# A two-layer decoder trunk on one core: when the first weight sums of a phase are fetched and split, and where two splits stand in a unit

## The chip, the cores and the metric

The kernel runs on one core of one Trainium2 chip. The metric is device time in microseconds, the median of several executions. The core has five engines that run side by side, each through its own instructions in a fixed order: TensorE (PE, matmuls), VectorE (DVE), ScalarE (ACT), GpSimd (POOL) and SyncE (SP). SP and POOL start DMA transfers here; an instruction that waits holds up everything behind it on its engine.

## The reference

The reference is a two-layer decoder trunk in float32 for one sequence of 256 tokens and a model width of 2048. Each layer has a token mixer and a gated MLP. The change lies in the MLP alone, which is

```python
h    = rmsnorm(x)
gate, val = h @ W_up                  # 2048 -> 2 x 5632
gate = silu(causal_conv3(gate))
y    = (gate * val) @ W_down          # 5632 -> 2048
x    = x + rmsnorm(y)
```

## The kernel before

**Precision.** PE multiplies a rounded float32. Each operand is therefore split in two: ACT copies it rounded into `hi` (L600), and DVE subtracts `hi` from it to give `lo` (L601). A product is three matmuls: hi·hi, lo·hi and hi·lo (`mm3`, L127). Weights arrive by DMA as float32 in a tile `raw` (three buffers for all uses) and are split into `whi` and `wlo` (four buffers each); the split's last subtraction lets the raw buffer go.

**The MLP of a layer.** The 5632 hidden columns are 11 groups of 512. Group 0 is done plainly (`narrow(0)`). Groups 1, 3, 5, 7 and 9 (`WIDE`) go through five wide phases per layer; each phase does two things side by side.

1. `wide` computes the two up projections of its group with seven products in place of eight (a Strassen scheme): L127 with the accumulators `ps_g` and `ps_s`. It runs over eight *units* (two 128-row blocks of the model width each). A unit needs four forms of weights. Two are plain and come from a 768 KB transfer `raw` (L637, from `uw`); `plain` splits them into `fa` (1024 columns) and `fb` (512 columns). Two are sums. The first sum `d` (`first_sums`, L606 and L607) is made by the transfer itself: SP loads 512 KB into a tile `sh`, and when that has landed POOL starts a second transfer of 512 KB that adds onto it. The second sum `e` is made by DVE from `d` and `raw` (L643, L644). Both are split into the four tiles called `x` (one buffer; L600 and L601 with `x<-sh`).
2. `beside` supplies one tile b of the plain up projection of the next group per unit (`ws_beside`, L155 to L175): a 1 MB transfer into `raw`, two splits of 1024 columns, two half sweeps of 16 matmuls (L162) into one PSUM bank, and then a copy on ACT (L174) and an addition on DVE (L175) that empty the bank. The first half sweep of the next tile cannot start before L175.

PE's order in unit u is fixed: first half sweep of b(u), products 1, 2 and 3 (9 matmuls, on `fa` and `fb`), second half sweep, products 7, 5, 6 and 4 (12 matmuls, on `x`). Instructions passed through `pin` keep the order in which the code issues them.

**Between phases** `downs` multiplies two finished groups by their down weights: eight 1 MB pieces (`dn`) of 24 matmuls each. The four results per layer half are stored to `yout` by POOL (from the second time on by an adding transfer, L764). In the middle of it `early(i)` requests the first sums of units 0 and 1 of the next phase. In phase 1 the request comes from `narrow(0)`, ahead of its second half.

Inside `wide`, unit u's code issues the loads and sums of unit u+1, and requests the first sums of unit u+2. Work left over from other parts (the convolution, SiLU and the gating) is called at `catch_up`.

**Order of the rest.** What is not pinned is placed by a scheduler, which works from the order of the code and its own costs; each engine's list is fixed once built. The list of an engine names tiles with a running number.

Of the kernel before, what the change touches and what calls it, by code (L numbers as in the profile page):

```python
# [10 lines left out]
F32 = mybir.dt.float32  # L11
# [25 lines left out]
WIDE = (1, 3, 5, 7, 9)  # L37
# [8 lines left out]
class Body:  # L46
    def __init__(self, ctx, tc, a):
        self.tc, self.nc, self.a = tc, tc.nc, a
        self.sb = ctx.enter_context(tc.tile_pool(name="sb", bufs=1))
        self.todo = []  # L50
        self.pinned, self.behind = False, []
        self.psp = ctx.enter_context(tc.tile_pool(name="ps", bufs=1, space=bass.MemoryType.PSUM))
        self.outside = ctx.enter_context(tc.tile_pool(name="outside", bufs=1, space=bass.MemoryType.DRAM))

# [45 lines left out]
    def piece(self, src, cuts=1, store=None, between=None):  # L100


        nc = self.nc
        raw = self.sb.tile([P, 2048], F32, name="raw", tag="raw", bufs=3)
        n = 2048 // cuts
        for h in range(cuts):
            dma = nc.sync.dma_start(raw[:, h * n:(h + 1) * n], src[:, h * n:(h + 1) * n])
            if cuts > 1:
                self.tc.keep_in_program_order(dma)
            if h == 0 and between:  # L110
                between()
        res = []
        n = min(n, 1024)
        for h in range(2):
            if store:
                hi, lo = (v[:, h * 1024:(h + 1) * 1024] for v in store)
            else:
                hi = self.sb.tile([P, 1024], F32R, name="whi", tag="whi", bufs=4)
                lo = self.sb.tile([P, 1024], F32R, name="wlo", tag="wlo", bufs=4)
            for i in range(0, 1024, n):  # L120
                r, ns = raw[:, h * 1024 + i:h * 1024 + i + n], slice(i, i + n)
                self.split(hi[:, ns], lo[:, ns], r)
            res.append((hi, lo))
        return res

    def mm3(self, out, lhi, llo, rhi, rlo, start, stop):
# [98 lines left out]
    def sums(self, n):  # L225

        ss = self.sb.tile([P, n, 5], F32, name="sums", tag="sums", bufs=2)
        self.nc.gpsimd.memset(ss[:, :, 4:5], EPS)
        return ss
# [367 lines left out]
        return s, make  # L597

    def split(self, hi, lo, of):
        self.pin(self.nc.scalar.copy(hi, of))  # L600
        self.pin(self.nc.vector.tensor_sub(lo, of, hi.bitcast(F32)))  # L601

    def first_sums(self, src, u):

# [3 lines left out]
                                 src[u][:, 1536:].unsqueeze(1).to_broadcast([P, 2, 512]), accum_op=ALU.add)  # L608
        return d

    def wide(self, src, ahead, h, s, forms, r, beside):

        nc, n = self.nc, KT // 2  # L620
        ps = {i: self.bank("g" if i in (1, 2, 6, 7) else "s") for i in range(1, 8)}
        pin, add = self.pin, nc.vector.tensor_add
        half = lambda f, i: f[..., i * 512:(i + 1) * 512]

        def lhs(i, u):
            if i in (1, 2, 4):
                kt, t = 2 * u + (i != 1), int(i == 4)
                return [h[2][:, kt, a, t * P:(t + 1) * P] for a in range(2)]
            return [s[:, u, {5: 0, 6: 1, 7: 2, 3: 3}[i], a, :] for a in range(2)]

        def product(i, u, f, at):
            self.mm3(ps[i], *lhs(i, u), half(f[0], at), half(f[1], at), u == 0, u == n - 1)

        def load(u):

            raw = self.sb.tile([P, 2048], F32, name="raw", tag="raw", bufs=3)
            nc.sync.dma_start(raw[:, :1536], src[u][:, :1536])  # L637
            return raw

        def sums(d, raw):  # L640

            e = self.sh([P, 1024])
            pin(add(half(e, 1), half(d, 0), half(raw, 2)))  # L643
            pin(add(half(e, 0), half(e, 1), half(raw, 0)))  # L644
            return d, e

        def plain(raw):
            fa, fb = ([self.sb.tile([P, 1024], F32R, name=k, tag=k, bufs=4) for k in ("whi", "wlo")]
                      for _ in range(2))
            self.split(*fa, raw[:, 0:1024])  # L650
            self.split(*(half(f, 0) for f in fb), half(raw, 2))
            return fa, fb

        summed = [[forms[:, 2 * i + j, :] for j in range(2)] for i in range(2)]

        def split_sums(t):
            for of, parts in zip(t, summed):
                self.split(*parts, of)

        raw = load(0)  # L660
        t = sums(ahead.pop(0), raw)
        split_sums(t)
        b = beside[0]()
        next(b)
        next(b)
        f = plain(raw)
        self.pinned = True
        for u in range(n):
            more = u + 1 < n
            next(b)  # L670
            if u:
                split_sums(t)
            self.catch_up()
            fa, fb = f
            product(1, u, fa, 1)
            product(2, u, fa, 0)
            product(3, u, fb, 0)
            if more:
                raw = load(u + 1)
                if u + 2 < n:  # L680
                    ahead.append(self.first_sums(src, u + 2))
                t, f = sums(ahead.pop(0), raw), plain(raw)
            self.catch_up()
            if more:
                after = beside[u + 1]()
                next(after)
            next(b)
            next(b, None)
            if more:
                next(after)  # L690
            product(7, u, summed[0], 1)
            product(5, u, summed[0], 0)
            product(6, u, summed[1], 1)
            product(4, u, summed[1], 0)
            b = after
        a, g0, v0, v1 = (self.sc([P, 512]) for _ in range(4))
        more = lambda out, x, i: pin(add(out, ps[i], x))

        def scaled(out, i, t):
            pin(nc.vector.scalar_tensor_tensor(out, ps[i], r[:, t:t + 1], out, op0=ALU.mult, op1=ALU.add))  # L700

        pin(nc.scalar.copy(a, ps[1]))
        pin(nc.scalar.activation(g0, ps[1], AF.Copy, scale=r[:, 0:1]))
        scaled(g0, 2, 0)
        more(a, a, 6)
        more(v0, a, 5)
        more(v0, v0, 3)
        more(a, a, 7)
        more(v1, a, 5)
        pin(nc.scalar.activation(a, a, AF.Copy, scale=r[:, 1:2]))  # L710
        scaled(a, 4, 1)
        self.pinned = False
        self.catch_up(-1)
        return (g0, a), (v0, v1)

    def ffn(self, layer, h, each, filler=None, done=None, late=None):
        nc = self.nc
        up, uw, dn = (self.a["%s%d" % (k, layer)] for k in ("up", "uw", "dn"))
        r, R = {}, []
# [23 lines left out]
        yout = self.outside.tile([4, P, 1024], F32, name="yout", tag="yout", bufs=1)  # L743
        acts, ahead = {}, []

        def early(i):
            ahead[:] = [self.first_sums(uw[i], u) for u in range(2)]

        def downs(groups):

            lhs = [p for b in groups for p in acts[b]]
            for c0 in (0, 2):
                banks = {c: [self.bank(), self.bank()] for c in (c0, c0 + 1)}
                for pi, b in enumerate(groups):
                    for c in banks:
                        self.as_piece(banks[c], dn[c, b:], lhs, pi, at=0)
                        if pi == 1:
                            y = self.sh([P, 1024])
                            for t in range(2):
                                nc.scalar.copy(y[:, t * 512:(t + 1) * 512], banks[c][t])  # L760
                            if 0 in groups:
                                nc.gpsimd.dma_start(yout[c], y)
                            else:
                                nc.gpsimd.dma_start(yout[c], y, accum_op=ALU.add)  # L764
                if c0 == 0:
                    early(WIDE.index(groups[1] + 1))

        def weights(ft):
            return [self.cols[:, cv + i * NFT + ft:cv + i * NFT + ft + 1] for i in range(4)]
# [58 lines left out]

        def narrow(g):
            for p in (2 * g, 2 * g + 1):  # L830
                if p % 2:
                    early(0)
                w = place(p)
                ga = self.ws_pair(up[w, 0], h)
                if p == 0:

                    val = self.ws_pair(up[w, 1], h)
                gate(ga)
                c, steps = conv(p, ga)
                at_once(steps)  # L840
                if p:
                    val = self.ws_pair(up[w, 1], h)
                at_once(keep(p, c, val))
# [46 lines left out]
        self.behind_this(*(lambda i=i: rest(i) for i in range(5, KT // 2 + 1)))  # L890
        forms = self.sb.tile([P, 4, 1024], F32R, name="x", tag="x", bufs=1)
        for g in WIDE:
            made = self.wide(uw[WIDE.index(g)], ahead, h, s, forms, R[0], beside(g + 1))
            for i in range(2):
                self.later(2 + i, lambda made=made, g=g, i=i: turned(g, made, i))
            if g < WIDE[-1]:
                downs((max(g - 2, 0), g + 1))
# [300 lines left out]
```

## Time and profile before

| | before |
|---|---|
| timed runs, us | 2294.56, 2297.04, 2300.41 (median 2297.04) |
| profiled execution, us | 2287.66 |
| its span, first to last instruction, us | 2285.9 |
| mean granted clock of PE | 0.986 |
| PE busy, us | 2212.9 (97%), 10962 matmuls |
| DVE busy, us | 1659.3 (73%) |
| ACT busy, us | 1304.1 (57%) |
| DMA moved | 516.78 MB, mean 226 GB/s |

How to read it: PE is the busiest engine by far, but its busy time is modelled and stretches with the clock, so what it waits for matters more than the share. A row of a timeline gives start, duration, engine, source line, operation, output and inputs, how often, and in square brackets the idle time before it and what ended that. A row of waits gives the waiting group, what released it, the total, the number of waits and the longest. In a row of windows the column after the length is PE's busy time, and the last three are the granted clock (1.00 is full), the busy share of the 16 DMA engines, and GB/s. A DMA row gives the issuing queue, the number of transfers, the size of one, and the median time from issue to landing.

### The profile page before, as it was taken

What the parts mean: (1) busy time and instruction counts of PE and PEld (TensorE: products, weight loads), DVE (VectorE), ACT (ScalarE), POOL (GpSimd) and SP (SyncE); (2) the same over time, 40 slices, a digit from 0 to 9 for tenths busy, and PEclk for the clock granted to TensorE, in tenths of its full rate; (3) what the DMA queues carried; (4) which work ended last, traced back from release to release, by engine and by line L of the source; (5) the groups of instructions that cost most, each with busy time, mean ns of one, the idle gap of its engine ahead of it and who ended that gap; (6) DMA issues with size and microseconds to landing.
All of it is one profiled execution on the core that took longest, in us unless ns stands there. A gap on an engine that the chain in (4) does not pass through costs nothing.

```text
span 2285.9 us, 28964 instructions
## 1 busy us (share of the span) xinstructions
PE 2212.9 (97%) x10962; PEld 1853.1 (81%) x10962; DVE 1659.3 (73%) x2175; ACT 1304.1 (57%) x1844; POOL 149.4 (7%) x168
## 2 busy tenths in 40 slices
PE   9999999999998999999999999999999999999998
PEld 7888888788787877778888888887877778787786
DVE  6567767987767858678864667579858678586786
ACT  7556556666555555556664555466555556555563
POOL 0000000101001010010000000001010010100100
PEclk9999999999999999999999999999999999999999
DMA  8755456877969688697755444658788786886974
GB/s 320 265 171 188 165 182 216 248 236 260 263 219 264 211 260 249 202 282 259 249 175 193 155 166 159 215 192 258 225 263 236 216 264 218 249 251 201 269 248 182
DMA packets 102380, 516.78 MB, mean 226 GB/s; under 512 B 10464, under 2 KB 10848, under 8 KB 61920
## 3 DMA queue, kind: packets, MB, share of 16 engines
q1 hardware_dynamic: 72288, 439.43, 54.3%
q0 software_dynamic: 29952, 75.51, 16.3%
q8 instruction: 86, 1.41, 0.2%
q14 instruction: 54, 0.44, 0.1%
HBM read 491.82 MB, written 23.07 MB: 225 GB/s over the span
## 4 chain that ended last, share of the span: by engine, by line
PE 79%; DMA 12%; DVE 4%; issue 2%; ACT 2%; SPq 0%; POOLq 0%; POOL 0%; DVEq 0%; ACTq 0%
PE ps_g L127 30%; PE ps_s L162 18%; DMA sh<-in_uw_dram 11%; PE ps_g L144 11%; PE ps_s L127 9%; PE ps_g L145 6%; DVE wlo L601 2%; ACT whi L600 1%; PE ps_g L147 1%; DMA raw<-in_up_dram 1%; PE ps_s L278 1%; DVE qk L785 1%; DMA raw<-in_wmv_dram 0%; ACT x L600 0%; PE ps_s L874 0%
## 5 line engine op out<-in xcount | busy, mean ns | idle before, releaser
L601 DVE TENSOR_TENSOR wlo<-raw,whi 128x1024 fp32r<-128x1024 f32 (+1 forms) x758 | 868.9, 1164 | 317.1 <-ACT whi L600 311.0
L600 ACT CAST whi<-raw 128x1024 fp32r<-128x1024 f32 (+1 forms) x758 | 757.5, 1004 | 503.2 <-PE ps_g L127 178.4
L162 PE MATMUL ps_s<-h,whi 128*128 128x512 f32 x1280 | 475.3, 406 | 31.4 <-DVE qk L175 31.4
L127 PE MATMUL ps_g<-whi,sh 128*128 128x512 f32 x1488 | 472.2, 399 | 18.6 <-ACT whi L600 18.6
L144 PE MATMUL ps_g<-h,whi 128*128 128x512 f32 x1200 | 431.3, 401 | 0.0
L162 PE MATMUL ps_s<-h,wlo 128*128 128x256 f32 x1280 | 352.4, 286 | 3.0 <-DVE wlo L601 3.0
L127 PEld LDWEIGHTS ps_g<-whi,sh 128*128 128x128 f32 x1488 | 282.2, 191 | 80.1 <-ACT whi L600 21.6
L145 PE MATMUL ps_g<-h,wlo 128*128 128x256 f32 x1280 | 346.1, 281 | 0.0
L162 PEld LDWEIGHTS ps_s<-h,whi 128*128 128x128 f32 x1280 | 247.0, 193 | 92.7 <-DVE qk L175 36.3
L127 PE MATMUL ps_g<-wlo,sh 128*128 128x512 f32 x744 | 296.7, 399 | 4.5 <-DVE wlo L601 4.5
L127 PE MATMUL ps_g<-whi,h 128*128 128x512 f32 x880 | 274.3, 393 | 1.7 <-ACT whi L600 1.7
L144 PEld LDWEIGHTS ps_g<-h,whi 128*128 128x128 f32 x1200 | 225.7, 188 | 51.4 <-DVE h L268 0.2
L162 PEld LDWEIGHTS ps_s<-h,wlo 128*128 128x128 f32 x1280 | 248.0, 194 | 14.1 <-DVE wlo L601 3.9
L601 DVE TENSOR_TENSOR x<-sh,x 128x1024 fp32r<-128x1024 f32 x160 | 192.0, 1222 | 79.6 <-ACT x L600 79.6
L145 PEld LDWEIGHTS ps_g<-h,wlo 128*128 128x128 f32 x1280 | 241.9, 189 | 6.3
L600 ACT CAST x<-sh 128x1024 fp32r<-128x1024 f32 x160 | 168.1, 1052 | 111.3 <-DMA sh<-in_uw_dram 89.2
L127 PEld LDWEIGHTS ps_g<-whi,h 128*128 128x128 f32 x880 | 159.4, 188 | 35.2 <-ACT whi L600 2.6
L127 PEld LDWEIGHTS ps_g<-wlo,sh 128*128 128x128 f32 x744 | 141.9, 191 | 40.8 <-DVE wlo L601 7.8
L127 PE MATMUL ps_g<-wlo,h 128*128 128x512 f32 x440 | 172.6, 393 | 1.1 <-DVE wlo L601 1.0
L607 POOL DMA_DIRECT2D sh<-in_uw_dram x80 | 96.0, 1200 | 669.3 <-DMA sh<-in_uw_dram 400.0
L127 PE MATMUL ps_g<-x,h 128*128 128x512 f32 x480 | 137.6, 394 | 0.0
L127 PE MATMUL ps_s<-x,h 128*128 128x512 f32 x480 | 137.2, 394 | 0.0
(180 smaller groups left out, 2029.9 us busy)
## 6 DMA issues: line engine op xcount, KB each, us to landing
raw<-in_up_dram SPq DMA_DIRECT2D x96, 1024.0 KB, 5.6
raw<-in_dn_dram SPq DMA_DIRECT2D x88, 1024.0 KB, 4.9
raw<-in_uw_dram SPq DMA_DIRECT2D x80, 768.0 KB, 7.2
sh<-in_uw_dram SPq DMA_DIRECT2D x80, 512.0 KB, 9.1
sh<-in_uw_dram POOLq DMA_DIRECT2D x80, 512.0 KB, 9.4
raw<-in_wqk_a_dram SPq DMA_DIRECT2D x24, 1024.0 KB, 4.8
yout<-sh POOLq DMA_DIRECT2D x32, 512.0 KB, 9.4
raw<-in_wo_b_dram SPq DMA_DIRECT2D x16, 1024.0 KB, 4.9
```

Of the source, the lines that this page charges most:

```text
L127: mm = lambda *o, **k: self.pin(self.nc.tensor.matmul(*o, **k))
L144: mm(b, whi[:, ks], both, start=kt == 0, stop=False)
L145: mm(b[:, 0:S], wlo[:, ks], one, start=False, stop=False)
L147: mm(b, whi[:, ks], both, start=False, stop=True)
L162: mm = lambda *o, **k: self.pin(self.nc.tensor.matmul(*o, **k))
L278: self.nc.tensor.transpose(b[:, k * S + t * P:k * S + (t + 1) * P], self.x[:, t, kt * P:(kt + 1) * P], self.ident)
L600: self.pin(self.nc.scalar.copy(hi, of))
L601: self.pin(self.nc.vector.tensor_sub(lo, of, hi.bitcast(F32)))
L607: self.nc.gpsimd.dma_start(d.rearrange("p (a n) -> p a n", a=2), src[u][:, 1536:].unsqueeze(1).to_broadcast([P, 2, 512]), accum_op=ALU.add)
L785: pin(nc.vector.scalar_tensor_tensor(c[:, j, d:], ga[:, j, :S - d], w[i], c[:, j, d:], op0=ALU.mult, op1=ALU.add))
```

## The change

`early` goes. The first sums of units 0 and 1 of the next phase are requested in units 6 and 7 of the phase ahead (`then`); those of phase 1 at the start of `narrow(0)`. The sums and splits of unit 0 are tied (`issue_after`) behind the split of the fourth piece from the end, which is the fifth of the eight down pieces. Within a unit the request for the first sums now stands ahead of the load of the next unit, and `plain`, the split of the two plain forms, moves from right behind the sums to behind the copy and addition that empty the tile b's bank.

```diff
-    def wide(self, src, ahead, h, s, forms, r, beside):
+    def wide(self, src, then, ahead, h, s, forms, r, beside):
...
         raw = load(0)
-        t = sums(ahead.pop(0), raw)
-        split_sums(t)
+
+        high, low = self.splits[-4]
+        with self.tc.issue_after(high.ins), self.tc.issue_after(low.ins):
+            t = sums(ahead.pop(0), raw)
+            split_sums(t)
...
             product(3, u, fb, 0)
+            if u + 2 < n:
+                ahead.append(self.first_sums(src, u + 2))
+            elif then is not None:
+                ahead.append(self.first_sums(then, u + 2 - n))
             if more:
                 raw = load(u + 1)
-                if u + 2 < n:
-                    ahead.append(self.first_sums(src, u + 2))
-                t, f = sums(ahead.pop(0), raw), plain(raw)
-            self.catch_up()
-            if more:
+                t = sums(ahead.pop(0), raw)
                 after = beside[u + 1]()
                 next(after)
+            self.catch_up()
             next(b)
             next(b, None)
             if more:
+                f = plain(raw)
                 next(after)
...
-        def early(i):
-            ahead[:] = [self.first_sums(uw[i], u) for u in range(2)]
...
-                if c0 == 0:
-                    early(WIDE.index(groups[1] + 1))
...
             for p in (2 * g, 2 * g + 1):
-                if p % 2:
-                    early(0)
+                if p == 0:
+                    ahead.extend(self.first_sums(uw[0], u) for u in range(2))
...
-            made = self.wide(uw[WIDE.index(g)], ahead, h, s, forms, R[0], beside(g + 1))
+            phase = WIDE.index(g)
+            then = uw[phase + 1] if g < WIDE[-1] else None
+            made = self.wide(uw[phase], then, ahead, h, s, forms, R[0], beside(g + 1))
```

`split` now returns its two instructions, and `piece` keeps those of its last split in the list `splits`. No operation is added or removed, and lines behind line 50 are numbered up to five higher than before.

SP's queue, the end of the second phase of layer 0 (`in_uw0` with L606/L608 are first sums, `raw<-in_up0` the tile b7, `in_dn0` the down pieces). Before:

```order
L606 DMA sh_5396<-in_uw0_dram 128x1024
L155 DMA raw_5497<-in_up0_dram 128x2048
L107 DMA raw_5623<-in_dn0_dram 128x2048
L107 DMA raw_5657<-in_dn0_dram 128x2048
L107 DMA raw_5718<-in_dn0_dram 128x2048
L107 DMA raw_5781<-in_dn0_dram 128x2048
L107 DMA raw_5829<-in_dn0_dram 128x2048
L107 DMA raw_5863<-in_dn0_dram 128x2048
L107 DMA raw_5897<-in_dn0_dram 128x2048
L107 DMA raw_5935<-in_dn0_dram 128x2048
L606 DMA sh_5819<-in_uw0_dram 128x1024
L606 DMA sh_5822<-in_uw0_dram 128x1024
```

And now:

```order
L608 DMA sh_5394<-in_uw0_dram 128x1024
L608 DMA sh_5482<-in_uw0_dram 128x1024
L156 DMA raw_5490<-in_up0_dram 128x2048
L107 DMA raw_5629<-in_dn0_dram 128x2048
L608 DMA sh_5574<-in_uw0_dram 128x1024
L107 DMA raw_5663<-in_dn0_dram 128x2048
```

The first row of either is d7 of the phase. The next phase's d0 and d1 stood behind the eight down pieces; now d0 stands right behind d7 and d1 behind the first down piece. POOL's two accumulations moved likewise, ahead of all four `yout` stores.

ACT's list, the last four down pieces of the same phase (`whi` of `raw_5863` and `raw_5897` are down pieces, `qk` and `sh` the convolution and gating, `x` the split of d0). Before:

```order
L600 CAST whi_5865<-raw_5863 128x1024
L789 ACTIVATE qk_5770<-qk_5770 128x512
L600 CAST whi_5869<-raw_5863 128x1024
L760 COPY sh_5815<-ps_g_5622 128x512
L809 CAST sh_5714<-qk_5770 128x512
L600 CAST whi_5899<-raw_5897 128x1024
L600 CAST whi_5903<-raw_5897 128x1024
L600 CAST x_3771<-sh_5819 128x1024
```

And now:

```order
L601 CAST x_3771<-sh_5482 128x1024
L601 CAST whi_5865<-raw_5863 128x1024
L792 ACTIVATE qk_5776<-qk_5776 128x512
L765 COPY sh_5821<-ps_g_5628 128x512
L601 CAST whi_5869<-raw_5863 128x1024
L812 CAST sh_5720<-qk_5776 128x512
L601 CAST whi_5899<-raw_5897 128x1024
L601 CAST whi_5903<-raw_5897 128x1024
```

The split of d0 stood ahead of the last down piece's casts; now it stands ahead of those of the last three.

DVE's list, from the sums of unit 1 of the next phase on (`raw_6035`, now `raw_6038`, is that unit's transfer; `raw_6051`, now `raw_6043`, the tile b1). Before:

```order
L643 TENSOR_TENSOR sh_6040<-sh_5822,raw_6035 128x512
L644 TENSOR_TENSOR sh_6040<-sh_6040,raw_6035 128x512
L601 TENSOR_TENSOR wlo_6044<-raw_6035,whi_6043 128x1024
L601 TENSOR_TENSOR wlo_6046<-raw_6035,whi_6045 128x512
L601 TENSOR_TENSOR wlo_6054<-raw_6051,whi_6053 128x1024
L175 TENSOR_TENSOR qk_5989<-ps_s_6009,qk_5989 128x256
L601 TENSOR_TENSOR wlo_6076<-raw_6051,whi_6075 128x1024
```

And now:

```order
L646 TENSOR_TENSOR sh_6040<-sh_5574,raw_6038 128x512
L647 TENSOR_TENSOR sh_6040<-sh_6040,raw_6038 128x512
L602 TENSOR_TENSOR wlo_6046<-raw_6043,whi_6045 128x1024
L176 TENSOR_TENSOR qk_5989<-ps_s_6009,qk_5989 128x256
L602 TENSOR_TENSOR wlo_6068<-raw_6038,whi_6067 128x1024
L602 TENSOR_TENSOR wlo_6070<-raw_6038,whi_6069 128x512
L602 TENSOR_TENSOR wlo_6076<-raw_6043,whi_6075 128x1024
```

The two subtractions of the plain forms stood ahead of the addition that empties the bank (L175, now L176); now they stand behind it. ACT's casts moved in the same way about its copy L174.

More of the change, by code (lines that the diff above doesn't have):

```diff
@@ L50, in __init__ @@
         self.todo = []
-        self.pinned, self.behind = False, []
+        self.pinned, self.behind, self.splits = False, [], []
         self.psp = ctx.enter_context(tc.tile_pool(name="ps", bufs=1, space=bass.MemoryType.PSUM))
@@ L121, in piece @@
                 r, ns = raw[:, h * 1024 + i:h * 1024 + i + n], slice(i, i + n)
-                self.split(hi[:, ns], lo[:, ns], r)
+                did = self.split(hi[:, ns], lo[:, ns], r)
             res.append((hi, lo))
+        self.splits.append(did)
         return res
@@ L599, in split @@
     def split(self, hi, lo, of):
-        self.pin(self.nc.scalar.copy(hi, of))
-        self.pin(self.nc.vector.tensor_sub(lo, of, hi.bitcast(F32)))
+        high = self.pin(self.nc.scalar.copy(hi, of))
+        low = self.pin(self.nc.vector.tensor_sub(lo, of, hi.bitcast(F32)))
+        return high, low
     def first_sums(self, src, u):
```

## The prediction

> **What bounds the kernel now.** I start with the page's chain of work that ended last, then the table of windows by stage, then the waits of TensorE (PE).
>
> ```profile
> PE ps_g L127 30%; PE ps_s L162 18%; DMA sh<-in_uw_dram 11%; PE ps_g L144 11%; PE ps_s L127 9%; PE ps_g L145 6%; DVE wlo L601 2%; ACT whi L600 1%; PE ps_g L147 1%; DMA raw<-in_up_dram 1%; PE ps_s L278 1%; DVE qk L785 1%; DMA raw<-in_wmv_dram 0%; ACT x L600 0%; PE ps_s L874 0%
> ...
> 407.00:1105.00 698.00, 672.18 (x3222) 558.14 (x3222) 535.51 (x662) 410.00 (x534) 66.26 (x66) 0.98 0.81 249
> 1105.00:1540.00 435.00, 432.64 (x2237) 367.16 (x2236) 290.51 (x405) 235.03 (x367) 7.88 (x14) 1.00 0.52 180
> 1540.00:2245.00 705.00, 672.30 (x3212) 557.28 (x3212) 530.23 (x654) 405.83 (x527) 66.23 (x66) 0.98 0.80 245
> ...
> PE ps_s L162 <- DVE qk L175: 31.4, 10, 5.2
> PE ps_g L127 <- ACT whi L600: 20.3, 9, 3.0
> PE ps_g L127 <- DVE wlo L601: 5.5, 9, 0.7
> PE ps_s L162 <- DVE wlo L601: 3.0, 2, 1.5
> ...
> POOL yout L764 <- ACT sh L760: 390.1, 24, 44.0
> ```
>
> The chain is matmuls but for one large piece, the transfer of first sums, `sh<-in_uw`, with 11%. The window rows show where it sits: the two stretches with wide phases are 698 and 705 us long with 672 us of PE in each (the column after the length), so PE stands idle 25.8 + 32.7 = 58.5 us there, while the attention between them idles 2.4. Behind the six busy columns stands the granted clock: 0.98, against 1.00. Two per cent of 1403 us is some 28 us more (0.975 to 0.985 as rounded: 21 to 35). The four waits name nearly the same idle time: 31.4 + 20.3 + 5.5 + 3.0 = 60.2 us. What this change can win at most is therefore 60 + 28 = 88 us; all else in these stretches is matmuls whose number stays.
>
> **Place B: the last down pieces, at seven of the eight changes of phase.**
>
> ```profile
> 676.18 9.91 DMA sh<-in_uw_dram
> ...
> 686.11 1.05 ACT L600 CAST x<-sh 128x1024 fp32r<-128x1024 f32 x1 [10.38 <-DMA sh<-in_uw_dram]
> ...
> 688.16 0.73 PE L127 MATMUL ps_g<-whi,sh 128*128 128x512 f32 x2 [2.29 <-ACT whi L600]
> ...
> 690.00:695.00 5.00, 5.00 (x17) 3.92 (x16) 4.26 (x5) 2.56 (x5) 0.90 (x1) 0.66 0.72 183
> ```
>
> ACT reaches the split of the next phase's d0 and sits 10.38 us until the accumulating transfer (begun 676.18) lands. The casts of the down pieces queue behind it, so PE waits for `whi`: 2.29 us, then some. Then the clock falls: 0.66 over 5 us, 0.34 x 5 = 1.7 us lost. The nine waits of either row above lie at seven places. Waits of 25.8 and seven times 1.7: **38 us**.
>
> **Place A: entry of unit 2 (unit 1 in a layer's first phase), all ten phases.**
>
> ```profile
> 693.37 9.65 DMA sh<-in_uw_dram
> ...
> 703.60 12.01 DMA sh<-in_uw_dram
> ...
> 715.63 0.69 DVE L643 TENSOR_TENSOR sh<-sh,raw 128x512 f32<-128x512 f32 x1 [6.50 <-DMA sh<-in_uw_dram]
> ...
> 716.97 2.96 DVE L601 TENSOR_TENSOR wlo<-raw,whi 128x1024 fp32r<-128x1024 f32 x3
> 719.84 0.42 DVE L175 TENSOR_TENSOR qk<-ps_s,qk 128x256 f32<-128x256 f32 x1
> 720.17 1.22 DVE L601 TENSOR_TENSOR wlo<-raw,whi 128x1024 fp32r<-128x1024 f32 x1
> ...
> 720.32 0.50 PE L162 MATMUL ps_s<-h,whi 128*128 128x512 f32 x1 [2.80 <-DVE qk L175]
> ...
> sh<-in_uw_dram SPq DMA_DIRECT2D x80, 512.0 KB, 9.1
> sh<-in_uw_dram POOLq DMA_DIRECT2D x80, 512.0 KB, 9.4
> ```
>
> d2's two legs (SP's at 693.37, POOL's at 703.60) end at 715.6. The sums of it, the two plain splits and one tile split go first, and L175, which frees the PSUM bank, is last. Of the 88 us, 31.4 + 28 - 7 x 1.7 = **47** are here, and 3 at a layer's first unit 0.
>
> **The change part by part.** Numbers of instructions and bytes stay; what moves is order.
>
> *First sums two units earlier, splits tied behind the fifth down piece.* d0 and d1 are now requested in units 6 and 7, some 50 us ahead of their first use, so ACT finds d0 landed, and nothing of place B remains: -38. The 3 us at unit 0 of a first phase go too, for the request stands ahead of the whole narrow group. POOL's and SP's queues now hold them ahead of the down pieces and the `yout` stores; those stores wait for ACT's copies, 390 us in 24 times (the first fence's last row), so this hides; without that cover a store would come one leg, some 9 us, later, which delays no matmul. What is late next is d2.
>
> *d2 in place A.* Its request still stands behind uw0, b0, uw1 and b1 on SP, so it moves earlier only as PE does (some 25.8 / 7 = 3.7 us with the waits of place B gone), and PE needs it earlier by as much. What is gained is the work ahead of L175: two of the three splits leave, 2.96 - 1.22 = 1.74 us. The transfers gain too: four legs of 512 KB no longer stand beside uw0 and b0. With both legs at the medians of all 80 (last two rows), 9.1 + 9.4 = 18.5 in place of 9.65 + 12.01 = 21.7, it is 3 us earlier. Of a mean wait of 3.1 us (31.4 in 10) 1.7 less leaves 1.4, and 4.9 less leaves nothing: I take 1.0 left per phase, with 0 and 2.3 as bounds, and 1.7 more for the clock at the upper one: 10 us left (0 to 40), so -37.
>
> A rule speaks on that end. In place A 2.80 us of idle were enough for the fall:
>
> ```profile
> 715.00:720.00 5.00, 2.52 (x11) 1.69 (x9) 4.33 (x6) 3.09 (x4) 0.42 (x1) 1.00 0.90 196
> 720.00:725.00 5.00, 4.68 (x18) 4.00 (x19) 4.97 (x7) 0.16 (x1) 0.77 (x1) 0.66 0.82 231
> ...
> 580.00:585.00 5.00, 2.57 (x15) 2.27 (x16) 5.00 (x7) 0.73 (x1) 1.21 (x1) 1.00 0.69 190
> 585.00:590.00 5.00, 5.00 (x29) 4.25 (x28) 4.97 (x7) 3.62 (x5) 0.00 (x0) 1.00 1.01 263
> ```
>
> A gap as long, at 580 to 585 (2.43 us without PE), kept 1.00. So a wait of 2.3 to 2.9 us falls on either side, and I price only the upper end with the clock. The Trainium skill (TensorE: Matmul & The Clock Gate, Part 1: The HAM clock gate) has the clock fall after one idle window of about 3.4 us. By that rule the upper end would be 23 and not 40 us; the first two rows here disagree, the last two agree.
>
> *Plain splits behind the tile's sum.* This adds a wait that the trace of before doesn't show. The `raw` tag has three buffers, and tile b(k+1) takes the one of uw(k). Before, uw(k) was let go by its plain splits right after its sums; now those stand behind L174/L175, and b(k+1) must land and be split before the next L174/L175. That is a loop from unit to unit.
>
> ```profile
> 613.98 0.39 PE L162 MATMUL ps_s<-h,whi 128*128 128x512 f32 x1
> ...
> 624.48 0.39 PE L162 MATMUL ps_s<-h,whi 128*128 128x512 f32 x1
> ...
> 618.15 3.02 DVE L601 TENSOR_TENSOR wlo<-raw,whi 128x1024 fp32r<-128x1024 f32 x3
> ...
> 622.30 0.43 DVE L175 TENSOR_TENSOR qk<-ps_s,qk 128x256 f32<-128x256 f32 x1 [1.13 <-ACT qk L174]
> ...
> 621.90 0.37 ACT L174 COPY qk<-ps_s 128x256 f32<-128x256 f32 x1 [1.98 <-PE ps_s L162]
> ...
> 623.12 1.05 ACT L600 CAST x<-sh 128x1024 fp32r<-128x1024 f32 x1
> ...
> raw<-in_up_dram SPq DMA_DIRECT2D x6, 1024.0 KB, 5.8
> ...
> raw<-in_up_dram SPq DMA_DIRECT2D x2, 1024.0 KB, 9.4
> ```
>
> A unit lasts 624.48 - 613.98 = 10.50 us. Once round the loop: the transfer, the cast of b's first half 1.05, L174 0.37, then the first plain cast 1.05 and its subtraction 1.22, and the small subtraction (3.02 less two of 1.22, about 0.6): 4.3, with issue 4.5, plus the transfer. It holds while b lands within 6.0 us. The median of 580 to 680 us is 5.8 (first of the two DMA rows), which just fits; at a phase's first units, 690 to 711, it is 9.4, which overruns by 3.4. The splits ahead of L175 were done at 621.17, 1.13 before L175 ran, so that much is forgiven: 2.3 lost if it happens once and nothing if the queue is as light as later. I take 1.5 per phase (0 to 3): **+15** (0 to 30).
>
> *d7 later.* SP holds d7 behind uw7, which takes b5's buffer, and b5's second split now stands behind the two plain ones.
>
> ```profile
> 614.39 0.87 SPq L606 DMA_DIRECT2D sh<-in_uw_dram  x1
> ...
> 620.37 1.18 POOL L607 DMA_DIRECT2D sh<-in_uw_dram  x1 [18.41 <-DVE wlo L601]
> ...
> sh<-in_uw_dram POOLq DMA_DIRECT2D x1, 512.0 KB, 7.9
> ...
> 628.34 0.69 DVE L643 TENSOR_TENSOR sh<-sh,raw 128x512 f32<-128x512 f32 x1 [0.93 <-DMA sh<-in_uw_dram]
> ```
>
> DVE already waits 0.93 for d7. The two splits push the request 1.8 us back, to 616.2: POOL 622.2 (5.98 later, as here), landed 630.1, sums 1.3, one split 1.2, and L175 could run at 632.7. The pace asks for 622.30 + 10.50 = 632.8: on time by a hair. With d0' and d1' now in the same queues I take 0.5 per phase (0 to 3): **+5** (0 to 30).
>
> *Layer 1's norm.* POOL's small operation for the second 128 tokens ran at 1504.12, and d0's accumulation now stands ahead of it, waiting for a request that goes out behind the transfer at 1494.05.
>
> ```profile
> 1494.05 0.33 SPq L107 DMA_DIRECT2D raw<-in_up_dram  x1
> ...
> 1504.12 0.57 POOL L237 TENSOR_TENSOR small<-small,mhalf 128x1 f32<-128x1 f32 x1 [1.32 <-DVE small L235]
> ```
>
> With the 9.1 above it lands at 1503.5, and POOL is late by 1 or 2 us, once: **+1** (0 to 5).
>
> Sum: -38 - 37 - 3 + 15 + 5 + 1 = **-57 us**. The profiled execution, 2287.66 us (span 2285.9), would become 2231. The three timed runs have a median of 2297.04, 9.4 above it; I take the loss from that: **2240 us**.
>
> **The rivals.**
> 1. *The loop becomes the bound; slower.* b's transfer competes with d's accumulation all the time now. Against it: medians of 5.8. For it: 9.4 where the queues are full. The point is 88 us over 70 unit changes, 1.26 each, so a mean landing of 7.3 us. At 7.5, (7.5 + 4.5 - 10.5) x 70 = 105, and 2297 - 88 + 105 = 2314. Chance 0.12. The Trainium skill (DMA: Bandwidth & Descriptors, Queues, rings and completion order) says that each DMA engine takes turns between the queues that have work, packet by packet; by that rule b slows whenever POOL's queue is busy beside it, and POOL's 12.01 beside 9.4 fits it.
> 2. *Place A stays.* d2's chain shifts with PE and only the 1.7 us per phase is won: -38 - 3 - 17 + 21 = -37, 2260. For it: the request's place on SP is unchanged. Chance 0.22.
> 3. *Nothing new is late.* Loop and d7 hide: 2297 - 88 = 2209, or 2219 with 10 left in place A. Chance 0.14.
> 4. *Moved, not won.* The first sums' transfers only delay units 6 and 7 and down pieces by what the phase start gains (5.5 us per phase more than I took): 2295. Chance 0.06.
>
> **How the numbers follow.** The forecast, 2240, has 0.46, with 2225 to 2255 its own range. The range 2207 to 2284 holds it, rivals 2 and 3, and part of what the bounds add (upper ends all at once would be 40 + 30 + 30 + 5 and so no gain). About 0.3% (7 us) is what a measurement of this kernel tells from no change: faster than 2290 has 0.82 (forecast, rivals 2 and 3), within it 0.06, slower 0.12.
>
> **What would show it.** Right: the wait of L127 for ACT's `whi` falls from 20.3 us to under 3; that of L162 for L175 from 31.4 to 10 to 30, spread over more and shorter places; the clock of both stretches is 0.99 or more; both shorten by 25 to 32 us. For rival 1: waits of L162 for L175 in most units, ACT's casts waiting for `raw<-in_up`. For rival 2: ten waits of 2 us or more at unit 2 behind `sh<-in_uw`. Wrong altogether would be a loss outside these stretches.

## The result, and the profile after

| | before | changed |
|---|---|---|
| timed runs, us | median 2297.47 (2294.56 to 2303.30) | median 2283.18 (2278.42 to 2286.25) |
| ratio of the medians | | 0.993, 95% interval 0.9909 to 0.9951 |
| profiled execution, us | 2287.66, span 2285.9 | 2280.21, span 2278.4 |
| mean granted clock | 0.986 | 0.991 |

The changed kernel is faster by 0.7%, some 14 us (7.5 us between the two profiled executions). 57 were forecast, and 2283 lies near the upper end of the range. A cost of nearly the size of the forecast gain must have come in.

From the changed kernel, the windows of the stretches with wide phases (length and PE's busy time first, the granted clock third from the end), and what PE waited for (total, number, longest):

```profile
407.00:1105.00 698.00, 668.02 (x3202) 553.03 (x3201) 527.24 (x657) 397.75 (x531) 63.39 (x64) 0.98 0.80 244
...
1540.00:2245.00 705.00, 677.60 (x3265) 560.43 (x3264) 535.36 (x666) 402.45 (x533) 63.39 (x64) 0.99 0.80 246
...
PE ps_s L163 <- DVE qk L176: 48.5, 24, 5.2
PE ps_g L128 <- ACT sc L711: 6.5, 10, 1.6
...
PE ps_g L128 <- DVE wlo L602: 1.0, 2, 0.5
...
PE ps_g L128 <- ACT whi L601: 0.5, 1, 0.5
```

The clock is 0.98 and 0.99, where 0.99 or more was expected of both stretches. From the start of a layer's first unit to the start of its last, PE took 632.5 and 642.0 us before and takes 634.9 and 629.3 now; each was to shorten by 25 to 32. The waits for `whi` and `wlo`, 25.8 us before, are 1.5. The wait of the half sweep (now L163) for the addition that empties its bank (now L176) did not fall from 31.4 to between 10 and 30; it rose to 48.5, and it now comes 24 times, not 10. The starts of PE's matmuls in the two traces say where. In this table, a start that comes later than the usual spacing allows (229 ns behind a matmul of 512 columns, 116 behind one of 256) counts with the excess, so that waits and slow-clock stretches are both in it:

| place | before, us | changed, us |
|---|---|---|
| B, last down pieces | 37 | 0 |
| A, entry of unit 2 (unit 1 in a first phase) | 48 | 13 |
| unit 0 of a first phase | 5 | 2 |
| other units of the first phases, 2 to 6 | 0 | 13 |
| end of unit 6 | 0 | 44 |
| first matmuls of the down pieces, waiting for copies of the products | 0 | 12 |
| sum | 90 | 84 |

The sums differ by 6 us, of the 7.5 between the two profiled executions. The change does what it says at A, B and unit 0: 75 us go. Some 69 come back, 44 of them at one place, the end of unit 6. There, in the second phase of layer 0 of the changed kernel, SP's requests (b6, uw7, then d7 and d0' in one row; b7, a down piece, d1'), POOL's, the DMA's own times for d7 (SP's leg, then POOL's), and what DVE and PE did:

```profile
623.46 0.33 SPq L156 DMA_DIRECT2D raw<-in_up_dram  x1
624.60 0.33 SPq L640 DMA_DIRECT2D raw<-in_uw_dram  x1
624.98 0.91 SPq L608 DMA_DIRECT2D sh<-in_uw_dram  x2
633.96 0.33 SPq L156 DMA_DIRECT2D raw<-in_up_dram  x1
635.10 0.33 SPq L107 DMA_DIRECT2D raw<-in_dn_dram  x1
635.48 0.79 SPq L608 DMA_DIRECT2D sh<-in_uw_dram  x1
...
sh<-in_uw_dram SPq DMA_DIRECT2D x1, 512.0 KB, 7.6
...
633.10 2.44 POOL L609 DMA_DIRECT2D sh<-in_uw_dram  x2 [17.67 <-DMA sh<-in_uw_dram]
...
sh<-in_uw_dram POOLq DMA_DIRECT2D x1, 512.0 KB, 11.4
...
633.34 0.39 PE L163 MATMUL ps_s<-h,whi 128*128 128x512 f32 x1
...
644.55 0.69 DVE L646 TENSOR_TENSOR sh<-sh,raw 128x512 f32<-128x512 f32 x1 [6.61 <-DMA sh<-in_uw_dram]
645.27 0.69 DVE L647 TENSOR_TENSOR sh<-sh,raw 128x512 f32<-128x512 f32 x1
645.88 1.22 DVE L602 TENSOR_TENSOR wlo<-raw,whi 128x1024 fp32r<-128x1024 f32 x1
647.02 0.42 DVE L176 TENSOR_TENSOR qk<-ps_s,qk 128x256 f32<-128x256 f32 x1
...
647.49 0.51 PE L163 MATMUL ps_s<-h,whi 128*128 128x512 f32 x1 [3.49 <-DVE qk L176]
```

The kernel before at the same place, SP's requests for b6 and uw7 and the time of d7's first leg:

```profile
609.50 0.33 SPq L155 DMA_DIRECT2D raw<-in_up_dram  x1
614.01 0.33 SPq L637 DMA_DIRECT2D raw<-in_uw_dram  x1
...
sh<-in_uw_dram SPq DMA_DIRECT2D x1, 512.0 KB, 5.4
```

Unit 6 starts at 633.34, and b6, uw7 and d7 were requested 9.9, 8.7 and 8.4 us ahead of it, within 1.5 us. Before, the same three went out at 609.50, 614.01 and 614.39 for a unit at 624.48: 15.0, 10.5 and 10.1 ahead. d7's first leg takes 7.6 and not 5.4. POOL can start the second only as the unit starts. It takes 11.4 and not 7.9: b7 and a down piece are now requested 0.9 and 2.0 us behind its start, where before b7 had gone out 0.4 us ahead of it (620.00) and the piece 4.1 behind (624.51). DVE gets d7 at 644.55 and waits 6.61 for it, L176 ends at 647.44, and PE has stood 3.49.

### The profile page after: what moved, and what is told of

It is laid out like the page before. It is cut to its first block, busy times and chain, and to the rows that moved or that the text cites. A ratio compares the mean times of both kernels' runs of the same rounds, so it can differ in the third digit from the quotient of the medians.

```text
span 2278.4 us, 28873 instructions
## 1 busy us (share of the span) xinstructions
PE 2206.8 (97%) x10962; PEld 1845.7 (81%) x10962; DVE 1651.4 (72%) x2175; ACT 1283.7 (56%) x1844; POOL 148.6 (7%) x168
## 4 chain that ended last, share of the span: by engine, by line
PE 78%; DMA 11%; DVE 5%; ACT 2%; issue 2%; SPq 0%; POOL 0%; POOLq 0%; ACTq 0%; DVEq 0%
PE ps_g L128 36%; PE ps_s L163 13%; PE ps_g L145 12%; PE ps_g L146 7%; DMA sh<-in_uw_dram 6%; PE ps_s L128 6%; DMA raw<-in_up_dram 4%; DVE wlo L602 3%; ACT whi L601 2%; PE ps_g L148 1%; PE ps_s L877 1%; DMA raw<-in_dn_dram 1%; PE ps_s L279 1%; DVE qk L176 0%; DMA raw<-in_wmv_dram 0%
## 5 line engine op out<-in xcount | busy, mean ns | idle before, releaser
L601 ACT CAST whi<-raw 128x1024 fp32r<-128x1024 f32 (+1 forms) x758 | 743.8, 1003 | 665.8 <-DMA raw<-in_up_dram 273.2
L163 PE MATMUL ps_s<-h,whi 128*128 128x512 f32 x1280 | 477.0, 408 | 48.5 <-DVE qk L176 48.5
L128 PE MATMUL ps_g<-whi,sh 128*128 128x512 f32 x1488 | 466.1, 394 | 7.9 <-ACT sc L711 6.5
L163 PE MATMUL ps_s<-h,wlo 128*128 128x256 f32 x1280 | 352.7, 286 | 0.0
L163 PEld LDWEIGHTS ps_s<-h,whi 128*128 128x128 f32 x1280 | 247.1, 193 | 115.5 <-DVE qk L176 59.8
L128 PEld LDWEIGHTS ps_g<-whi,sh 128*128 128x128 f32 x1488 | 276.6, 188 | 71.4 <-ACT sc L711 10.9
L128 PE MATMUL ps_g<-wlo,sh 128*128 128x512 f32 x744 | 292.0, 393 | 0.0
L163 PEld LDWEIGHTS ps_s<-h,wlo 128*128 128x128 f32 x1280 | 248.4, 194 | 9.6
L601 ACT CAST x<-sh 128x1024 fp32r<-128x1024 f32 x160 | 161.4, 1049 | 9.0 <-DMA sh<-in_uw_dram 6.9
```

Source lines behind the costliest of these rows:

```text
L128: mm = lambda *o, **k: self.pin(self.nc.tensor.matmul(*o, **k))
L163: mm = lambda *o, **k: self.pin(self.nc.tensor.matmul(*o, **k))
L601: high = self.pin(self.nc.scalar.copy(hi, of))
```

## The experiments

T is the theory that the moved plain splits bunch the requests and make d7 late. R, its rival, is that the next phase's d0' and d1', now requested in units 6 and 7, crowd d7 out. All times are medians, ratios are to the kernel before, and the last two columns are the time beyond spacing, as in the table above, at the end of unit 6 and at place A (in kernels 3 and 9 the first phases' units 1 to 3 are all counted).

| kernel | median, us | ratio, 95% interval | unit 6 | A |
|---|---|---|---|---|
| changed | 2283.18 | 0.9930 (0.9909 to 0.9951) | 44 | 13 |
| 1 plain splits back | 2238.75 | 0.9728 (0.9702 to 0.9755) | 0 | 42 |
| 2 first sums back | 2325.27 | 1.0109 (1.0075 to 1.0143) | 47 | |
| 3 late in units 1 and 2 | 2222.96 | 0.9664 (0.9635 to 0.9693) | 12 | 18 |
| 4 first sums behind b7 | 2291.23 | 0.9963 (0.9935 to 0.9991) | 53 | |
| 5 late but in unit 6 | 2277.27 | 0.9922 (0.9899 to 0.9945) | 50 | |
| 6 late in unit 6 alone | 2244.12 | 0.9775 (0.9755 to 0.9794) | 2 | 44 |
| 7 late in unit 2 alone | 2229.48 | 0.9706 (0.9680 to 0.9732) | 2 | |
| 8 late in unit 5 alone | 2306.13 | 1.0038 (1.0023 to 1.0054) | 69 | 39 |
| 9 late at place A alone | 2226.24 | 0.9681 (0.9664 to 0.9698) | 1 | 26 |

**1. The plain splits back, the early first sums kept.**

```diff
-                t = sums(ahead.pop(0), raw)
+                t, f = sums(ahead.pop(0), raw), plain(raw)
...
-                f = plain(raw)
```

> The plain splits stand right behind the sums again, as before; the early requests and the tie stay. Theory T (the moved plain splits hold the raw buffers longer, so that b(k+1), uw(k+2) and d are requested in one bunch and d7's accumulation lands late): the overrun at the end of unit 6 (44 us with the slow clock behind it, over nine phases) falls under 8, the long units of each layer's first phase (15 us) go, and place A grows by some 1.7 us per phase, 15 to 30 us in all. Time 2235 to 2260. Rival R (d0' and d1' of the next phase crowd d7 out): the overruns at unit 6 stay over 30 us, time 2283 or more.

Measured 2238.75. No unit 6 overruns, the long units of the first phases are gone, and so are the waits of the down pieces for copies. PE's waits:

```profile
PE ps_s L163 <- DVE qk L176: 25.8, 10, 4.0
PE ps_s L279 <- DVE x L528: 2.1, 1, 2.1
PE ps_g L128 <- ACT whi L601: 1.3, 2, 1.0
```

Place A is back with ten waits, worth 42 us with the clock, against 48 in the kernel before and 13 in the changed one. So the early first sums with their tie are worth 59 us alone (2297 to 2239). The moved splits win some 29 at A and lose 69 elsewhere.

**2. The first sums back in the middle of the down pieces, without the tie; the plain splits moved.**

```diff
+                if c0 == 0:
+                    i = WIDE.index(groups[1] + 1)
+                    ahead.extend(self.first_sums(uw[i], u) for u in range(2))
...
-        high, low = self.splits[-4]
-        with self.tc.issue_after(high.ins), self.tc.issue_after(low.ins):
-            t = sums(ahead.pop(0), raw)
-            split_sums(t)
+        t = sums(ahead.pop(0), raw)
+        split_sums(t)
...
-            elif then is not None:
-                ahead.append(self.first_sums(then, u + 2 - n))
```

(`narrow` requests those of phase 1 ahead of its second half again.)

> The first sums of the next phase are requested in the middle of the down pieces again, without the tie; the plain splits stay moved. T: unit 6 overruns stay (30 us or more) and the waits of place B return (some 38 us): 2310 to 2330. R: the overruns at unit 6 are gone, place B is back: 2270 to 2285.

Measured 2325.27: slower than the kernel before. Unit 6 overruns by 47 us with none of the next phase's sums in flight, and place B is back with 36. R can't be the cause. Unit 0 of layer 1's first phase loses 9 us here, against 3 before; why stays open.

**3. Plain splits late for units 1 and 2 only.**

```diff
                 t = sums(ahead.pop(0), raw)
+                if not (u < 2):
+                    f = plain(raw)
...
-                f = plain(raw)
+                if u < 2:
+                    f = plain(raw)
```

> The plain splits stand behind the tile's sum only for units 1 and 2, and right behind the sums for units 3 to 7; early requests and tie stay. T: unit 6 overruns under 8 us, no long units in the first phases beyond unit 2, place A as short as in the changed kernel (about 10 us): 2220 to 2240. R: overruns at unit 6 stay, 2270 to 2285.

Measured 2222.96, 3.4% faster than before and 2.6% faster than the changed kernel. Unit 6 still overran in three phases of ten: 12 us, where under 8 were expected. There too d7's second leg is the long one, 10.6 to 11.0 us against 6.4 to 9.2 in the other seven; late splits of unit 5 are not at work here, so they are not the only way to such an overrun.

**4. d0' and d1' requested at the start of the down pieces' code, behind b7.**

```diff
             lhs = [p for b in groups for p in acts[b]]
+            i = WIDE.index(groups[1] + 1)
+            ahead.extend(self.first_sums(uw[i], u) for u in range(2))
...
-            elif then is not None:
-                ahead.append(self.first_sums(then, u + 2 - n))
```

> d0' and d1' are requested at the start of the down pieces' code, behind the tile b7, in place of units 6 and 7; the plain splits stay moved. T: unit 6 overruns as in the changed kernel (over 30 us with the slow clock), since the fifth phase of layer 0 overruns by 5 us with no d0' at all: 2275 to 2295. R: overruns at unit 6 go: 2235 to 2250.

Measured 2291.23, with 53 us at unit 6. Moving the next phase's transfers out of the way of d7's first leg doesn't help, as T has it.

**5 and 6. Which unit's splits?** In 5 those of unit 6 alone stand right behind the sums, in 6 they alone stand late. The edit is that of 3 with `u != 5` and `u == 5` for `u < 2`.

> As the changed kernel, but the plain splits of unit 6 alone (issued in unit 5) stand right behind the sums. Theory U (those two splits alone do it: they hold uw6's buffer, which b7 takes, and push back b5's second split, which frees uw7's buffer, with d7 behind it): overruns at unit 6 under 8 us, the waits of the next down pieces for the result copies gone, long units of the first phases and the short place A stay: 2220 to 2242. Rival V (all units of a phase run bunched, and d7 is late because of the units ahead): overruns at unit 6 stay at 20 us or more, 2255 to 2285.

> The plain splits of unit 6 alone stand behind the tile's sum; those of all other units stand right behind the sums; early requests and tie stay. U: overruns at unit 6 of 30 us or more, place A as with the plain splits back (about 35 us): 2270 to 2295. V: little or nothing more than with the plain splits back: 2238 to 2255.

Measured 2277.27 and 2244.12. U, my own guess, falls by both runs: without that unit's late splits the overruns stay (50 us), and with them alone there are 2. The trace of the sixth kernel says why. Second phase of layer 0, SP's requests (b6, uw7, d7 with d0'; b7), POOL's, the two legs of d7, and unit 6's first matmul:

```profile
609.11 0.33 SPq L156 DMA_DIRECT2D raw<-in_up_dram  x1
613.61 0.33 SPq L640 DMA_DIRECT2D raw<-in_uw_dram  x1
613.99 1.12 SPq L608 DMA_DIRECT2D sh<-in_uw_dram  x2
624.71 0.33 SPq L156 DMA_DIRECT2D raw<-in_up_dram  x1
...
sh<-in_uw_dram SPq DMA_DIRECT2D x1, 512.0 KB, 5.5
...
620.01 2.43 POOL L609 DMA_DIRECT2D sh<-in_uw_dram  x2 [18.37 <-DMA sh<-in_uw_dram]
...
sh<-in_uw_dram POOLq DMA_DIRECT2D x1, 512.0 KB, 6.1
...
624.09 0.39 PE L163 MATMUL ps_s<-h,whi 128*128 128x512 f32 x1
```

d7 is on time, 10.1 us ahead, and its second leg takes 6.1, with b7 4.7 us behind it. Unit 6's late splits hold back b7 and what follows it, not d7. What holds back uw7 and d7 is b5's second split, and that stands behind the plain splits of unit *5*, which also keep b6's buffer.

**7. Late for unit 2 alone** (`u == 1`).

> The plain splits of unit 2 alone stand behind the tile's sum. U and V alike: no overrun at unit 6, no long units in the first phases, place A short in eight phases (it lies at unit 1 in a layer's first phase, where some 2 us more stay each): 2212 to 2230.

Measured 2229.48, as expected; it can't be told from 3, whose interval overlaps.

**8. Late for unit 5 alone** (`u == 4`). W is the reading of the requests just given.

> The plain splits of unit 5 alone (issued in unit 4) stand behind the tile's sum; early requests and tie stay. Theory W, from the requests in the traces: these hold back b6 and, by b5's second split, uw7 and d7 behind it; d7 goes out about 8.4 us ahead of unit 6 and not 10.1, in one bunch with b6 and uw7, its first leg takes 7 to 8 us and not 5.4, and POOL starts the second beside unit 6's entry, not 4 us ahead; with b7 already under way that leg takes 11 us. Overruns at unit 6 of 25 us or more, place A as with the plain splits back: 2265 to 2285. Theory V (all units together): no more than 10 us of overruns, 2238 to 2250.

Measured 2306.13: one pair of splits in one unit of eight costs 67 us against kernel 1, more than expected. The same rows as above, with DVE's and PE's wait:

```profile
617.37 0.33 SPq L156 DMA_DIRECT2D raw<-in_up_dram  x1
618.51 0.33 SPq L640 DMA_DIRECT2D raw<-in_uw_dram  x1
618.89 0.92 SPq L608 DMA_DIRECT2D sh<-in_uw_dram  x2
624.45 0.33 SPq L156 DMA_DIRECT2D raw<-in_up_dram  x1
...
sh<-in_uw_dram SPq DMA_DIRECT2D x1, 512.0 KB, 6.9
...
626.31 1.18 POOL L609 DMA_DIRECT2D sh<-in_uw_dram  x1 [21.95 <-DVE qk L176]
...
sh<-in_uw_dram POOLq DMA_DIRECT2D x1, 512.0 KB, 11.7
...
627.24 0.39 PE L163 MATMUL ps_s<-h,whi 128*128 128x512 f32 x1
...
638.03 0.69 DVE L646 TENSOR_TENSOR sh<-sh,raw 128x512 f32<-128x512 f32 x1 [7.87 <-DMA sh<-in_uw_dram]
...
642.71 0.80 PE L163 MATMUL ps_s<-h,whi 128*128 128x512 f32 x1 [4.81 <-DVE qk L176]
```

b6, uw7 and d7 are 9.9, 8.7 and 8.4 us ahead of the unit (627.24), the very distances of the changed kernel, and POOL starts 0.9 ahead and not 4. PE stands 4.81 and not 3.49, since here unit 7's plain splits stand ahead of L176 again. W holds and V falls: unit 5's late splits are enough by themselves. Units 3, 4 and 7 were not tried alone. R has a part in the size in this kernel: in the two phases with no next phase in their layer (no d0', d1') the second leg took 8.4 and 8.7 us and the overrun is some 4 us each, in the other eight 10.1 to 11.8 and 6 to 8. The changed kernel shows nothing of the kind: its fifth phase of layer 0, without d0' and d1', has a leg of 10.6 and an overrun of 5.

**9. Late only where place A lies** (unit 1 in a layer's first phase, unit 2 in the others; the phase is kept in `self.phase`, the condition is `u == min(self.phase, 1)`).

> The plain splits stand behind the tile's sum only where place A lies: unit 1 in a layer's first phase, unit 2 in the others; right behind the sums elsewhere. W: no overrun at unit 6 to speak of (under 8 us), place A short everywhere: 2215 to 2228, no slower than the two kernels that do it for units 1 and 2 or for unit 2 alone (2223 and 2229). V says the same.

Measured 2226.24, within the expected range, and not to be told from 3 and 7. Unit 6 is clean. In place A 26 us stay, twice the 13 of the changed kernel; why stays open.

## Why the prediction was wrong

Its sign was right, its size was not: 57 forecast, 14 measured. By its own terms:

- **Place B, -38.** Right: 37 before, nothing now. ACT's split of the sums waits for their transfer 6.9 us in all, from 89.2 before.
- **Place A, 10 us left of 47.** Right: 13 of 48, and rival 2, that A stays, fell. Of its two parts only one is borne out. The moved splits' 1.7 us per phase are there: kernel 1's ten waits of 25.8 us are some 10 in the changed kernel. The 3 us that less crowded transfers were to give are 0.6, for the early requests alone bring 31.4 to 25.8. That 1.0 left per phase, a choice between the two ends, came out is in part luck.
- **Unit 0 of a first phase, -3.** Right (5 to 2).
- **The buffer loop, +15.** The size was right, 13, the place wrong, so the size is luck. I put it at the start of every phase, from a median of 9.4 us of two transfers of b. It sits in the first phases of both layers, in unit after unit, and the other phases show next to nothing. In phase 1 of layer 1 of the changed kernel b takes 7 to 8 us (first row), ACT's cast waits for it, and the unit is 12 us long (1596.05 to 1608.20, 1608.20 to 1620.98):

```profile
raw<-in_up_dram SPq DMA_DIRECT2D x1, 1024.0 KB, 8.0
...
1618.29 1.05 ACT L601 CAST whi<-raw 128x1024 fp32r<-128x1024 f32 x1 [6.63 <-DMA raw<-in_up_dram]
...
1596.05 0.50 PE L163 MATMUL ps_s<-h,whi 128*128 128x512 f32 x1 [1.12 <-DVE qk L176]
1608.20 0.50 PE L163 MATMUL ps_s<-h,whi 128*128 128x512 f32 x1 [1.37 <-DVE qk L176]
1620.98 0.60 PE L163 MATMUL ps_s<-h,whi 128*128 128x512 f32 x1 [2.05 <-DVE qk L176]
```

  By the prediction's own rule, landing plus 4.5, a landing of 8.0 gives 12.5, and the unit that it lies in is 12.8 long: the rule comes close. Why only the first phases settle into this pace stays open.
- **d7, +5 (0 to 30).** This is the step that failed: 44, and it is outside its own bounds. The text had it on time "by a hair" at 632.7 (its terms add up to 632.6) against 632.8. Its first part, that the request comes 1.8 us later because b5's second split does, was right (10.1 to 8.4 us ahead, 1.7; kernel 8 shows the path). Then it took the legs from a trace in which b6 had gone out 4.5 us ahead of uw7 and stood out of d7's way: "5.98 later, as here", and 7.9. In the changed kernel they are 633.10 - 624.98 = 8.1 and 11.4, so 2.1 and 3.5 more, because the same moved splits change what the legs run beside: b6 goes out 1.5 us ahead of d7 and not 4.9, and b7 and a down piece now follow the second leg's start by 0.9 and 2.0. An edit had been priced with latencies that the edit itself changes.
- **The copies at the down pieces, 12 us**, were no term at all. Kernel 1, with the plain splits back, hasn't got them, and neither have kernels 3, 7, 8 and 9, so late splits in units 1, 2 or 5 don't bring them. Kernel 6, late in unit 6 alone, has some 3, kernel 5, late in all others, some 6, and kernel 4, late in all with the sums requested behind b7, some 20. What delays the copies stays open.
- **Layer 1's norm, +1.** Nothing: POOL's two small operations are 5.53 us apart in both traces (1498.59 and 1504.12, now 1502.43 and 1507.96).

Of the rivals, number 4 (gains lost again in units 6 and 7, 2295, chance 0.06) came nearest in time and place, but its cause, the next phase's sums, was refuted by kernel 2, and kernel 4 agrees. Rival 1 named transfers that slow each other, b's and the accumulation, but put the loss into every unit.

## What to carry to other kernels

A request held back by a shared buffer was late twice here: by the wait itself, and because it then went out in one bunch with what it used to follow, and the later transfers of the bunch took longer (uw7 6.7 us for 4.6, d7's first leg 7.6 for 5.4). So price a moved release by listing which requests will now leave together, and don't take their latencies from the trace in which they left apart. And where an edit that helps one unit is applied in all, try it in that unit alone: kernels 3, 7 and 9 keep the gain and are 2.4 to 2.6% faster than the changed one.

## What the runs showed of the hardware

I had treated the time of the accumulating transfer of 512 KB as a property of the transfer. d7's took 6.1 to 12.5 us in the ten phases of the changed kernel, and the number of transfers beside it does not decide it alone. In eight phases b7 went out within 1.2 us of its start: 9.1 to 12.5. In the other two it started 1.5 and 1.7 us ahead of b7 and took 6.4 and 6.1, though a down piece followed too. These are the rows of the last phase, POOL's start, the time it took, b7 and the piece:

```profile
2177.32 1.19 POOL L609 DMA_DIRECT2D sh<-in_uw_dram  x1 [16.29 <-DMA sh<-in_uw_dram]
...
sh<-in_uw_dram POOLq DMA_DIRECT2D x1, 512.0 KB, 6.1
...
2178.99 0.33 SPq L156 DMA_DIRECT2D raw<-in_up_dram  x1
2180.12 0.33 SPq L107 DMA_DIRECT2D raw<-in_dn_dram  x1
```

This phase has no overrun, though d7 is requested 8.3 us ahead of unit 6, no earlier than in the second phase (8.4). With b7 0.4 us ahead of it and the piece 4.1 behind it took 8.0 (kernel 1, second phase). A second accumulation 1.2 us behind it on POOL didn't slow it: 6.1 with one and 6.2 without (kernel 6, second and fifth phase). Why so small a lead matters is not shown.

The clock's fall is not fixed by the length of the wait. Kernel 1 waited 2.67 us and kept full clock over the next 5 us; kernel 3 waited 1.85 and fell to 0.68 (each wait's row, and the window behind it, clock third from the end):

```profile
709.06 0.50 PE L163 MATMUL ps_s<-h,whi 128*128 128x512 f32 x1 [2.67 <-DVE qk L176]
...
709.00:714.00 5.00, 4.94 (x25) 4.24 (x26) 4.96 (x7) 1.68 (x3) 1.20 (x1) 1.00 0.86 292
...
1605.34 0.50 PE L163 MATMUL ps_s<-h,whi 128*128 128x512 f32 x1 [1.85 <-DVE qk L176]
...
1605.00:1610.00 5.00, 4.66 (x18) 4.00 (x19) 4.95 (x7) 0.56 (x1) 0.61 (x1) 0.68 0.80 230
```
